# Attention on one core: the two parts of an output block are added by an accumulating DMA instead of by a Pool addition

## The chip, the cores and the metric

The kernel runs on one core of a Trainium2 chip. The core has TensorE (PE, matrix products), VectorE (DVE), ScalarE (ACT), GpSimd (Pool) and SyncE (SP), and 16 DMA engines that they share. SP and Pool both issue DMAs; a DMA that changes the type or accumulates is issued by Pool here. The metric is device time in microseconds. The kernel before takes 794.21 us, the median of three runs (793.92 to 794.26).

## The reference

For each of 8 batches the kernel computes softmax(q kT / sqrt(512)) v, in float32, with 2048 rows and 512 columns:

```python
scores = np.matmul(q, k.transpose(0, 2, 1)) / np.sqrt(d_k)
attn_weights = special.softmax(scores, axis=-1).astype(np.float32)
return np.matmul(attn_weights, v)
```

## The kernel before

*Tiling.* Each batch is worked through in four steps, g = 4b to 4b + 3, so g runs from 0 to 31. In a step TensorE computes half of the scores of the next span of 1024 query rows (class Group, product at L342) and, interleaved with that, the product of weights and values for four blocks of 128 output rows (classes Pair, L447, and Fine, L634). Both products use Strassen's scheme: seven block products in place of eight, with sums and differences of blocks made ahead by VectorE (L194 to L197 for k, L211 to L214 for q, L395 to L398 and L588 to L591 for the weights). For g = 1 to 29 the products named x, y and z of a pair are themselves done by an inner Strassen scheme, the function fine.

*Output.* Each Fine object has four quarters of its output: C11, C12, C21, C22, here o11, o12, o21 and o22, each 128 rows by 256 columns in float32. They are tiles of one pool of eight buffers (opool). ScalarE writes a quarter from PSUM with the row's factor (scaled, L456). For o11, there are two parts: the one from x is written to o11 by part(), and the one from y is written to a second tile, more, by after2(). Pool adds more to o11 at L555, and SP stores o11 to DRAM (store, L469). There are 58 of these additions: two in each of the steps g = 1 to 29. A step takes ten tiles of the pool. 

*Loads.* For the next batch, chunks of 512 rows of k, q and v are loaded by Pool's DMAs with a change from float32 to float16: k and q into a pool of two stage tiles (load, L133), v straight to its place (L220). SP transposes a stage tile into its place by a DMA transpose (L159). The transposed chunk of k is then summed by VectorE, L194 first (k_sums; the word k01 in the table is the first of the four sums for chunk 0).

*Order.* The order of everything is written out by hand. A step has 34 slots, and tables say what is put into each: PRODUCTS (t3@25 and t4@27 end in after2 for the pairs a and b), SUMS (k01@11 in the second step of a batch) and PLAN for loads and transposes:

```python
(0, 18, "load", "k", 0), (1, 0, "trans", "k", 0),
(0, 24, "load", "k", 1), (1, 8, "trans", "k", 1),
```

The first two numbers are the step of the batch and the slot. So on Pool the order around the end of a batch's first step is: load k0, load k1, addition a, addition b. On SP it is: store of o11 of a, store of o11 of b, transpose of k0, the stores of the o22 and o21 quarters, transpose of k1. Every engine works in the order in which its instructions were issued. An engine waits on semaphores where its data come from another engine or a DMA; these waits are put in by the framework.

Of the kernel before, what the change touches and what calls it, by code (L numbers as in the profile page):

```python
# [12 lines left out]
def kernel(  # L13
# [21 lines left out]
    nc = tc.nc  # L35
# [7 lines left out]
    ADD = mybir.AluOpType.add  # L43
# [266 lines left out]
    class Group:  # L310
# [61 lines left out]
        def after2(self):  # L372
            exp(self.left[0][:, self.j, :], self.y[:])
# [147 lines left out]
    class Fine(Pair):  # L521
# [29 lines left out]
        def after2(self):  # L551
            if "y" in INNER(self.g) and self.g < NP - 2:
                more = self.half()
                self.scaled(more, self.y[:, 0:H], self.r1)
                nc.gpsimd.tensor_add(self.o11, self.o11, more)  # L555
                self.store(self.o11, 0, slice(0, H))
                return
            if "y" in INNER(self.g):
                self.final(self.o11, self.y[:, 0:H], self.r1)
            else:  # L560
                self.o11 = self.half()
                self.scaled(self.o11, self.y[:, 0:H], self.r1)
            self.store(self.o11, 0, slice(0, H))
# [114 lines left out]
    def INNER(g):  # L678
        return INNERS[g % NQT] if 0 < g < NP - 2 else END_INNERS.get(g, "")
# [251 lines left out]
    for g in range(NP):  # L931
# [3 lines left out]
        more = sp < NP // 2  # L935
# [53 lines left out]
```

## Time and profile before

| What | Value |
|---|---|
| time, median of three runs (range) | 794.21 us (793.92 to 794.26) |
| profiled execution: span on the core | 792.4 us; the page gives no other time for it |
| busy: TensorE, VectorE, ScalarE, Pool | 786.1, 712.4, 646.3, 124.1 us |
| granted TensorE clock | 1.000 |
| HBM read, written | 100.73 MB, 33.55 MB |
| additions at L555 | 58, together 51.1 us of Pool |

The span runs from the first to the last instruction on the core. A row of a group has the line, the engine, the operation, the tiles (output, arrow, inputs), the shapes and the count; behind the bar stand the busy time in us, the mean of one in ns, and the idle time of the engine just before, with what ended it. A row of the timeline has the start in us, the duration in us, engine and line, and in brackets the idle time before and what ended it; instructions of the same kind that follow each other are merged, with their count. A row of the DMA issues has the count, the size of one and the median time in us from issue to landing. A queue's row has packets, megabytes, and the time that its packets took as a share of 16 engines over the span. In the waits, a row has the total in us, the count and the longest.

### The profile page before, as it was taken

Reading aid. Unit: us, or ns where it says so; the run is one execution under the profiler, and the core shown is the slowest. Engines: PE = TensorE matmul, PEld = TensorE weight load, DVE = VectorE, ACT = ScalarE, POOL = GpSimd, SP = SyncE. Lnnn points to the kernel's source line nnn. Section 1 sums busy time; section 2 is a strip of 40 time slices with the busy share of each in tenths; the row PEclk is TensorE's granted clock in tenths of the full one; section 3 lists DMA queues with packets and bytes.
Section 4 is the critical chain, followed back from the end, with each engine's and each line's share of the span. In section 5 each row is a group of like instructions: output and inputs, shape, how many; then the busy total and the mean of one; then the engine's idle time right before and its main releaser. Section 6 shows DMA issues by size and latency. Waiting matters only on the chain.

```text
span 792.4 us, 17987 instructions
## 1 busy us (share of the span) xinstructions
PE 786.1 (99%) x6574; PEld 536.6 (68%) x6574; DVE 712.4 (90%) x1562; ACT 646.3 (82%) x1339; POOL 124.1 (16%) x166
## 2 busy tenths in 40 slices
PE   9999999999999999999999999999999999999998
PEld 5556666666666666666666676666666666666686
DVE  3789999989999899998999989999899998999864
ACT  4678888888888888888988888888888888888862
POOL 4011111121121120211202121022210222100000
PEclk9999999999999999999999999999999999999999
DMA  9989991999929996399965999379991999911112
GB/s 222 180 149 187 159 192 35 175 199 166 180 43 186 209 176 134 71 195 180 172 130 106 193 189 180 82 136 200 163 202 55 151 195 178 195 35 47 49 66 95
DMA packets 206456, 116.05 MB, mean 146 GB/s; under 512 B 124320, under 2 KB 205344, under 8 KB 206368
## 3 DMA queue, kind: packets, MB, share of 16 engines
q0 software_dynamic: 49648, 49.29, 42.2%
q1 hardware_dynamic: 156432, 65.30, 39.0%
q8 instruction: 51, 0.84, 0.4%
q10 hardware_dynamic: 288, 0.33, 0.1%
q14 instruction: 37, 0.30, 0.1%
HBM read 100.73 MB, written 33.55 MB: 169 GB/s over the span
## 4 chain that ended last, share of the span: by engine, by line
PE 96%; DVE 2%; ACT 1%; issue 1%; DVEq 0%; ACTq 0%
PE t L342 45%; PE t L447 29%; PE t L634 17%; PE t L285 2%; DVE cz L367 1%; DVE ks L196 1%; PE tr L169 1%; PE tr L146 0%; PE t L853 0%; PE t L301 0%; DVE right L397 0%; ACT right L278 0%; ACT o L456 0%; ACT left L278 0%; DVE s L396 0%
## 5 line engine op out<-in xcount | busy, mean ns | idle before, releaser
L456 ACT ACTIVATE o<-t,r 128x256 f32<-128x256 f32 x314 | 143.9, 480 | 88.0 <-DVE r L482 33.2
L342 PE MATMUL t<-qraw,kraw 128*128 128x512 f16 x728 | 198.0, 379 | 0.1
L278 ACT ACTIVATE left<-t 128x512 f16<-128x512 f32 (+1 forms) x260 | 154.4, 601 | 12.0 <-PE t L342 5.8
L342 PE MATMUL t<-qs,ks 128*128 128x512 f16 x488 | 138.7, 379 | 0.1
L278 ACT ACTIVATE right<-cz 128x1024 f16<-128x1024 f32 x122 | 129.9, 1065 | 1.0 <-DVE cz L364 0.8
L342 PEld LDWEIGHTS <-kraw 128*128 128x128 f16 x976 | 87.1, 97 | 57.9 <-issue 0.6
L447 PEld LDWEIGHTS <-right 128*128 128x128 f16 x1024 | 99.5, 98 | 38.3 <-DVE right L397 2.7
L447 PEld LDWEIGHTS <-s 128*128 128x128 f16 x1072 | 102.1, 97 | 30.5 <-issue 0.3
L634 PEld LDWEIGHTS <-si 128*128 128x128 f16 x1044 | 75.4, 97 | 39.4 <-issue 1.4
L555 POOL TENSOR_TENSOR o<-o 128x256 f32<-128x256 f32 x58 | 51.1, 882 | 307.9 <-ACT o L456 221.2
L367 DVE TENSOR_TENSOR cz<-t,cz 128x512 f32<-128x512 f32 x122 | 83.8, 686 | 15.3 <-ACT o L456 6.7
L342 PEld LDWEIGHTS <-ks 128*128 128x128 f16 x732 | 67.9, 97 | 40.2 <-issue 0.2
L358 ACT COPY cz<-t 128x512 f32<-128x512 f32 x120 | 70.5, 587 | 26.2 <-PE t L342 25.2
L364 DVE TENSOR_TENSOR cz<-t,cz 128x512 f32<-128x512 f32 x122 | 83.5, 684 | 4.0 <-PE t L342 3.6
L634 PEld LDWEIGHTS <-left 128*128 128x128 f16 x928 | 66.2, 97 | 20.6
L459 DVE SCALAR_TENSOR_TENSOR o<-t,r,o 128x256 f32<-128x256 f32 x134 | 62.5, 478 | 19.0 <-ACT ci L652 6.4
L353 ACT COPY t<-t 128x512 f32<-128x512 f32 x120 | 69.9, 583 | 3.2 <-PE t L342 0.8
L447 PE MATMUL t<-vt,s 128*128 128x256 f16 (+1 forms) x560 | 72.5, 273 | 0.0
L342 PE MATMUL t<-qs,kraw 128*128 128x512 f16 x244 | 72.5, 378 | 0.0
L342 PE MATMUL t<-qraw,ks 128*128 128x512 f16 x244 | 72.4, 378 | 0.0
L361 ACT COPY cz<-t 128x512 f32<-128x512 f32 x122 | 71.2, 583 | 0.3
L634 PE MATMUL t<-vh,left 128*128 128x128 f16 x696 | 67.3, 219 | 0.0
(101 smaller groups left out, 1239.1 us busy)
## 6 DMA issues: line engine op xcount, KB each, us to landing
out_dram<-o SPq DMA_DIRECT2D x256, 128.0 KB, 2.5
vh<-in_v_dram POOLq DMA_DIRECT2D x32, 512.0 KB, 10.6
stage<-in_q_dram POOLq DMA_DIRECT2D x28, 512.0 KB, 7.1
stage<-in_k_dram POOLq DMA_DIRECT2D x28, 512.0 KB, 7.6
right<-in_q_dram POOLq DMA_DIRECT2D x2, 512.0 KB, 9.9
right<-in_k_dram POOLq DMA_DIRECT2D x2, 512.0 KB, 12.0
first<-in_q_dram SPq DMA_DIRECT2D x2, 256.0 KB, 3.7
cz<-in_q_dram SPq DMA_DIRECT2D x2, 256.0 KB, 4.7
```

The source lines that it names most:

```text
L278: nc.scalar.activation(out=out_, in_=in_, func=EXP, scale=inv_sqrt_d)
L342: nc.tensor.matmul(dst[:], lhs[:, j, dc, :], rhs[:, :, dc, :], start=(n in (1, 5) and dc == 0), stop=(dc == 1), skip_group_check=True,)
L353: f(out=self.y[:], in_=self.x[:])
L358: f(out=self.cz[:, 1, :], in_=self.z[:])
L361: nc.scalar.copy(out=self.cz[:, 0, :], in_=self.x[:])
L364: nc.vector.tensor_add(self.cz[:, 1, :], self.x[:], self.cz[:, 1, :])
L367: nc.vector.tensor_add(self.cz[:, 0, :], self.z[:], self.cz[:, 0, :])
L447: nc.tensor.matmul(dst[:, 0:width], lhs(j), rhs(j), start=(first and j == 0), stop=(j == NJ - 1), skip_group_check=True,)
L456: nc.scalar.activation(out=out_, in_=src, func=COPY, scale=r[:])
L459: nc.vector.scalar_tensor_tensor(out=out_, in0=src, scalar=r[:], in1=out_, op0=MULT, op1=ADD)
L555: nc.gpsimd.tensor_add(self.o11, self.o11, more)
L634: nc.tensor.matmul(dst, lhs[:, j, :], rhs[:, j, :], start=(n == 1 and j == 0), stop=(j == NI - 1), skip_group_check=True,)
```

## The change

In after2 the Pool instruction that adds more to o11 is replaced by a DMA that Pool issues. It reads more from SBUF, reads o11, and writes the sum to o11, in float32.

```diff
             if "y" in INNER(self.g) and self.g < NP - 2:
                 more = self.half()
                 self.scaled(more, self.y[:, 0:H], self.r1)
-                nc.gpsimd.tensor_add(self.o11, self.o11, more)
+                nc.gpsimd.dma_start(out=self.o11, in_=more, accum_op=ADD)
                 self.store(self.o11, 0, slice(0, H))
                 return
```

ADD is the addition that the kernel names at its start. The store that follows is issued by SP as before. Nothing else differs.

## The prediction

> **What bounds the kernel now.** I read the page's busy times and its chain first, then the row of the edited line, and after that the order in time on Pool, SP and VectorE around one of the edited places.
>
> ```profile
> span 792.4 us, 17987 instructions
> PE 786.1 (99%) x6574; PEld 536.6 (68%) x6574; DVE 712.4 (90%) x1562; ACT 646.3 (82%) x1339; POOL 124.1 (16%) x166
> PE 96%; DVE 2%; ACT 1%; issue 1%; DVEq 0%; ACTq 0%
> L555 POOL TENSOR_TENSOR o<-o 128x256 f32<-128x256 f32 x58 | 51.1, 882 | 307.9 <-ACT o L456 221.2
> ```
>
> TensorE is busy for 786.1 of 792.4 us and makes 96% of the chain. So at most 792.4 - 786.1 = 6.3 us could be won anywhere, and whatever stops TensorE is lost for good, for it has no idle time to catch up in. The 58 additions to be replaced (L555) take 51.1 us of Pool, which is 16% busy and not in the chain: taking them away is worth nothing by itself. The question is whether the accumulating DMA ends later than the addition did, and who stands behind it. The profiled execution has a span of 792.4 us; the median of the runs is 794.21, so 1.8 us lie around the span, and I add changes to 794.2.
>
> Who waits for L555 is seen in SP's own waits, and what SP does next in its timeline. This is the boundary between g = 8 and g = 9; g counts the groups of output rows, four to a batch, and I call them steps. Rows: start, duration, engine, line, operation, and in brackets the idle time before.
>
> ```profile
> SPq L469 <- POOL o L555: 68.8, 50, 2.6
> ...
> 250.41 7.04 SPq L469 DMA_DIRECT2D out_dram<-o  x4
> 257.56 3.81 SPq L159 DMA_TRANSPOSE kraw<-stage  x1
> 261.46 1.50 SPq L469 DMA_DIRECT2D out_dram<-o  x3
> ```
> ```profile
> 250.16 0.75 POOL L133 DMA_DIRECT2D stage<-in_k_dram  x1 [14.49 <-DMA qraw<-stage]
> 252.00 0.74 POOL L133 DMA_DIRECT2D stage<-in_k_dram  x1 [1.09 <-DMA qraw<-stage]
> 255.10 0.86 POOL L555 TENSOR_TENSOR o<-o 128x256 f32<-128x256 f32 x1 [2.36 <-issue]
> 256.18 0.92 POOL L555 TENSOR_TENSOR o<-o 128x256 f32<-128x256 f32 x1 [0.22 <-ACT o L456]
> ```
> ```profile
> 263.80 0.43 DVE L589 TENSOR_TENSOR si<-si,left 128x512 f16<-128x512 f16 x1
> 264.14 0.42 DVE L194 TENSOR_TENSOR ks<-kraw 128x512 f16<-128x512 f16 x1
> 265.53 0.69 DVE L367 TENSOR_TENSOR cz<-t,cz 128x512 f32<-128x512 f32 x1 [0.98 <-ACT o L456]
> ```
>
> Pool issues the loads of two key chunks (k0 at 250.16, k1 at 252.00), then makes the two additions. SP stores both sums, the last of the four stores before 257.56, and only then transposes k0. VectorE's first sum over k0 (L194) runs at 264.14, with no idle time ahead of it. The next rows are the landing times of k0's load, k1's load and k0's transpose.
>
> ```profile
> stage<-in_k_dram POOLq DMA_DIRECT2D x1, 512.0 KB, 7.3
> stage<-in_k_dram POOLq DMA_DIRECT2D x1, 512.0 KB, 8.8
> kraw<-stage SPq DMA_TRANSPOSE x1, 5.8
> ```
>
> k0's load lands at 250.16 + 7.3 = 257.5, and the transpose starts at 257.56: it lands at 263.4, and L194, which needs it, starts 0.8 us later. This is a chain without slack: load, transpose, sum.
>
> **The change part by part.** *Removed:* 58 Pool additions of 882 ns. *Added on Pool:* 58 DMA issues; the 512 KB loads above cost Pool 0.75 us each, so Pool is held about as long as before, and its later loads start as before: 0. *The sum of an output half* is no longer there 0.9 us after ScalarE wrote its second part, but when the DMA has landed. *SP's store* now waits for that landing, with everything behind it on SP: the other half's store, the transpose, the stores of the o22 and o21 halves.
>
> *When does it land?* Pool's DMAs all show as one queue, q0. Three loads, issued 0.76 us apart, show how it is served:
>
> ```profile
> 327.55 2.00 POOL L555 TENSOR_TENSOR o<-o 128x256 f32<-128x256 f32 x2 [21.86 <-ACT o L456]
> 329.50 1.52 POOL L133 DMA_DIRECT2D stage<-in_q_dram  x2
> 331.00 0.76 POOL L220 DMA_DIRECT2D vh<-in_v_dram  x1
> ```
> ```profile
> stage<-in_q_dram POOLq DMA_DIRECT2D x1, 512.0 KB, 6.5
> ...
> stage<-in_q_dram POOLq DMA_DIRECT2D x1, 512.0 KB, 9.8
> vh<-in_v_dram POOLq DMA_DIRECT2D x1, 512.0 KB, 12.7
> ```
>
> They land at 329.5 + 6.5 = 336.0, 330.3 + 9.8 = 340.1 and 331.0 + 12.7 = 343.7: one after the other, 4 us apart, not together. So the two accumulating DMAs, issued at about 255.1 and 256.2, stand behind k1's load, which lands at 252.00 + 8.8 = 260.8, 3.7 us after the last addition ended in the old kernel (256.18 + 0.92).
>
> *What does one take by itself?* No row shows an accumulating DMA. The queues' totals give the nearest packets:
>
> ```profile
> q0 software_dynamic: 49648, 49.29, 42.2%
> q1 hardware_dynamic: 156432, 65.30, 39.0%
> ```
>
> On q0 a packet of about 1 KB takes 0.422 x 16 x 792.4 / 49648 = 0.108 us, on q1 (smaller ones too) 0.032. An output half is 128 rows of 1 KB, 8 for each of 16 engines: 0.86 us at q0's price, 0.25 at q1's. Reading two operands and writing one without overlap may cost three times the first: 2.6. I take 0.86: it is Pool's own queue with rows of the same length; the ends are 0.25 and 2.6.
>
> *The sum for one place.* The transpose of k0 would start when k1's load has landed, plus two accumulating DMAs, plus the last store's issue (1.50 / 3 = 0.5 us by the row at 261.46). From that go the slack of L194 and the idle time of VectorE just after it, which takes up delay (0.98 us at 265.53). There are six such places, g = 4, 8, ... 24 with the next one (g = 0 has no L555, the last batch loads nothing). The first and the last of them, each with its k1 load, transpose, L194 and the L367 after it:
>
> ```profile
> 156.60 0.74 POOL L133 DMA_DIRECT2D stage<-in_k_dram  x1 [1.11 <-DMA qraw<-stage]
> ...
> stage<-in_k_dram POOLq DMA_DIRECT2D x1, 512.0 KB, 9.1
> ...
> 161.23 4.65 SPq L159 DMA_TRANSPOSE kraw<-stage  x1
> ...
> kraw<-stage SPq DMA_TRANSPOSE x1, 6.7
> ...
> 167.95 0.43 DVE L194 TENSOR_TENSOR ks<-kraw 128x512 f16<-128x512 f16 x1
> 169.16 0.69 DVE L367 TENSOR_TENSOR cz<-t,cz 128x512 f32<-128x512 f32 x1 [0.79 <-ACT o L456]
> ```
> ```profile
> 636.97 0.74 POOL L133 DMA_DIRECT2D stage<-in_k_dram  x1 [1.02 <-ACT cz L358]
> ...
> stage<-in_k_dram POOLq DMA_DIRECT2D x1, 512.0 KB, 7.6
> ...
> 641.97 3.29 SPq L159 DMA_TRANSPOSE kraw<-stage  x1
> ...
> kraw<-stage SPq DMA_TRANSPOSE x1, 6.8
> ...
> 648.84 0.43 DVE L194 TENSOR_TENSOR ks<-kraw 128x512 f16<-128x512 f16 x1 [0.21 <-DMA kraw<-stage]
> 649.94 0.69 DVE L367 TENSOR_TENSOR cz<-t,cz 128x512 f32<-128x512 f32 x1 [0.68 <-ACT o L456]
> ```
>
> k1's landing less the transpose's old start: 165.7 - 161.23 = 4.5, 260.8 - 257.56 = 3.2, 644.6 - 641.97 = 2.6; mean 3.4. Slack of L194: 0.0, 0.8, 0.1; mean 0.3; in the last place the sum waits for the transpose already. Idle time after it: 0.8, 1.0, 0.7; mean 0.8. So VectorE falls behind by 3.4 + 2 x 0.86 + 0.5 - 0.3 - 0.8 = 4.5 us in each place. What it does next (L367 and its like) frees the PSUM banks that TensorE writes, so I pass the whole delay on; a few tenths may be absorbed. 6 x 4.5 = 27; I take 26 for that and forecast 794.2 + 26 = 820 us. At the low end of the DMA's price the place costs 3.3 us (814), at the high end 8.0 (842).
>
> A page of the Trainium skill prices a transfer otherwise: "DMA: Bandwidth & Descriptors", section "Anatomy of one DMA — SWDGE (gpsimd) path", gives a DMA issued by Pool 2.0 us fixed and the bytes at 436 GB/s. By that one half would be 2.3 us, and if the fixed part were paid one after the other the forecast would be some 17 us higher, 837 (an estimate from that page). The rows above have no accumulating DMA to test it; three whole loads 4 us apart leave both open.
>
> *The other boundaries* are taken at 0. At the end of g = 9 no load is in the queue, so SP waits some 2 or 3 us longer; the chunk that is transposed next is summed half a step later. At the end of g = 10 a load of v is ahead, and the next transpose is one of q, read a step later. At the end of g = 11 (327.55) the two DMAs stand ahead of the three loads at 329.50: they put k0's chain off by up to 1.7 us if the queue is full, which would add 10 in all. The cover is that the queue was empty before them, so they run before the loads' packets come. *The output buffers*: ten halves are taken in a step and eight exist. ScalarE would stop if a store came so late that a half is not free; the stores behind the transpose are 6 us late. No DMA is among the rows that ScalarE waits for now, so I take 0, and with the slow DMA above it adds to the high end.
>
> **The rivals.**
> *The accumulating DMA is slow* (2.0 us or more each): 4.5 + 2 x (2.0 - 0.86) = 6.8 us in six places, 835, and 842 at 2.6; more if ScalarE runs out of output halves. For it speaks that reading the destination is new work; against it nothing in the trace. It begins to decide at about 1.5 us.
> *It does not stand behind the load:* packets of the two mix, and it lands some 3.5 us after issue (between the median 2.5 us of a 128 KB store to DRAM and the 6.5 us of a load).
>
> ```profile
> out_dram<-o SPq DMA_DIRECT2D x256, 128.0 KB, 2.5
> ```
>
> Then the transpose starts at 256.18 + 3.5 + 0.5 = 260.2, 2.6 late; less 0.3 and 0.8 that is 1.5 us, six times 9: 803. The three landings 4 us apart speak against it.
> *Hidden:* TensorE's and VectorE's leads take the whole delay: 794. Against it stands L194 with its slack of 0.0 to 0.8 us.
> *Faster:* Pool's additions read memory beside VectorE and slow it; without them VectorE is earlier and TensorE's last gaps close. At most the 6.3 us go, 788; it would decide if the SP wait cost under that. The page "SBUF — State Buffer" of the Trainium skill, section "Who interferes with whom", states such a shared port for VectorE instructions with two inputs in SBUF. The trace speaks against a gain that counts: VectorE is not what the chain runs over (2%).
>
> **How the numbers follow.** Chances: forecast 0.65, slow DMA 0.15, not behind the load 0.12, hidden 0.05, faster 0.03. The time is the first one's, 820; its own range, by the price of one DMA, is 810 to 832. The range for all, 802 to 842, takes in the rival at 803 and the bound at 842 and leaves about 2 in 10 out: hidden, faster, and the worse half of slow. What a measurement can tell from no change is 0.2%, 1.6 us: faster 0.03, same 0.05, slower 0.92.
>
> **What would show it.** In the new profile: SP's longest waits at L469 are for a DMA into o, of 5 to 8 us, six times; k0's transpose starts 5 to 6 us later against its load; VectorE shows idle time before L194 ended by the DMA kraw<-stage, some 4 to 5 us each, 25 to 30 in all; TensorE loses as much just after. The DMA's landing time is 6 to 8 us where a load is ahead, 3 to 4 elsewhere. Wrong would be: no wait before L194 (hidden or mixed), waits of ScalarE for out_dram stores (buffers), or a delay at every step and not at one in four (the DMA itself is slow).

## The result and the profile after

The changed kernel takes 818.59 us (median; 814.52 to 825.45) against 794.07 of the kernel before beside it: a ratio of 1.0317, with a 95% interval of 1.0268 to 1.0366. It is slower by some 25 us, inside the range of the forecast and 1.4 us from its number. The profiled execution has a span of 818.1 us, 25.7 more than before.

From the page and the list of waits (total in us, count, longest):

```profile
span 818.1 us, 18007 instructions
PE 792.2 (97%) x6574; PEld 542.7 (66%) x6574; DVE 697.7 (85%) x1562; ACT 645.1 (79%) x1339; POOL 124.2 (15%) x166
q0 software_dynamic: 58000, 56.90, 47.6%
PE 93%; DMA 4%; DVE 1%; ACT 1%; issue 0%; SPq 0%; ACTq 0%
L555 POOL DMA_DIRECT2D o<-o x58 | 50.4, 878 | 297.8 <-ACT o L456 263.5
```
```profile
DVE ks L194 <- DMA kraw<-stage: 31.4, 6, 7.4
PE t L634 <- DVE si L591: 20.4, 6, 5.5
SPq L469 <- DMA o<-o: 176.9, 50, 10.5
```

The chain now has 4% of DMA in it. VectorE waits six times for the transpose of k (31.4 us in all, 0.2 before), and TensorE six times for VectorE just after (20.4 us). Pool is held by a DMA issue about as long as by an addition, 878 ns against 882. One number goes the other way: VectorE is busy for 14.7 us less than before, with the same 1562 instructions.

The boundary between g = 8 and g = 9, in the timelines of Pool, SP, VectorE and TensorE:

```profile
255.34 0.74 POOL L133 DMA_DIRECT2D stage<-in_k_dram  x1 [2.83 <-DMA qraw<-stage]
256.08 1.82 POOL L555 DMA_DIRECT2D o<-o  x2
...
251.87 13.61 SPq L469 DMA_DIRECT2D out_dram<-o  x4
265.59 2.02 SPq L159 DMA_TRANSPOSE kraw<-stage  x1
...
271.53 0.42 DVE L194 TENSOR_TENSOR ks<-kraw 128x512 f16<-128x512 f16 x1 [7.38 <-DMA kraw<-stage]
...
273.68 0.61 PE L634 MATMUL t<-vh,si 128*128 128x128 f16 x4 [5.54 <-DVE si L591]
```

The DMA rows of that place are k1's load, the two accumulating DMAs and k0's transpose; then follow k0's transposes of the first and the fourth of the six places; the last row is an accumulating DMA at the end of a fourth step, with no load ahead of it:

```profile
stage<-in_k_dram POOLq DMA_DIRECT2D x1, 512.0 KB, 8.4
o<-o POOLq DMA_DIRECT2D x2, 128.0 KB, 8.4
kraw<-stage SPq DMA_TRANSPOSE x1, 5.9
...
kraw<-stage SPq DMA_TRANSPOSE x1, 4.2
kraw<-stage SPq DMA_TRANSPOSE x1, 4.3
...
o<-o POOLq DMA_DIRECT2D x1, 128.0 KB, 2.7
```

k1's load lands at 255.34 + 8.4 = 263.7. The accumulating DMAs were issued at 256.1 and 256.8 and land 8.4 us later, at 264.5 and 265.1: one after the other behind the load, 0.7 us each. Alone one takes 2.7 us. SP's store waits, the transpose starts at 265.59, and L194 waits 7.38 us for it.

### The profile page after: what moved, and what is told of

Its sections match the earlier page's. It is cut to its first block, busy times and chain, and to the rows that moved or that the text cites. A ratio compares the mean times of both kernels' runs of the same rounds, so it can differ in the third digit from the quotient of the medians.

```text
span 818.1 us, 18007 instructions
## 1 busy us (share of the span) xinstructions
PE 792.2 (97%) x6574; PEld 542.7 (66%) x6574; DVE 697.7 (85%) x1562; ACT 645.1 (79%) x1339; POOL 124.2 (15%) x166
## 4 chain that ended last, share of the span: by engine, by line
PE 93%; DMA 4%; DVE 1%; ACT 1%; issue 0%; SPq 0%; ACTq 0%
PE t L342 44%; PE t L447 30%; PE t L634 16%; DMA kraw<-stage 3%; PE t L285 2%; PE tr L169 1%; DMA first<-in_q_dram 1%; DVE cz L367 1%; PE t L301 0%; PE tr L146 0%; DVE left L590 0%; DVE si L591 0%; DVE t L658 0%; ACT left L278 0%; ACT right L278 0%
## 5 line engine op out<-in xcount | busy, mean ns | idle before, releaser
L342 PE MATMUL t<-qraw,kraw 128*128 128x512 f16 x728 | 198.1, 379 | 0.1
L342 PE MATMUL t<-qs,ks 128*128 128x512 f16 x488 | 141.7, 386 | 0.0
L342 PEld LDWEIGHTS <-kraw 128*128 128x128 f16 x976 | 87.3, 98 | 58.4 <-issue 1.7
L447 PEld LDWEIGHTS <-s 128*128 128x128 f16 x1072 | 104.5, 99 | 31.7 <-issue 0.9
L342 PEld LDWEIGHTS <-ks 128*128 128x128 f16 x732 | 68.9, 99 | 41.4 <-issue 2.6
L555 POOL DMA_DIRECT2D o<-o x58 | 50.4, 878 | 297.8 <-ACT o L456 263.5
L364 DVE TENSOR_TENSOR cz<-t,cz 128x512 f32<-128x512 f32 x122 | 83.8, 687 | 6.7 <-PE t L342 5.9
L634 PEld LDWEIGHTS <-left 128*128 128x128 f16 x928 | 68.3, 100 | 21.1
L342 PE MATMUL t<-qs,kraw 128*128 128x512 f16 x244 | 73.1, 381 | 0.0
L342 PE MATMUL t<-qraw,ks 128*128 128x512 f16 x244 | 72.5, 379 | 0.0
L447 PE MATMUL t<-vh,s 128*128 128x257 f16 x512 | 71.6, 285 | 0.0
```

The source lines that it names most:

```text
L342: nc.tensor.matmul(dst[:], lhs[:, j, dc, :], rhs[:, :, dc, :], start=(n in (1, 5) and dc == 0), stop=(dc == 1), skip_group_check=True,)
L364: nc.vector.tensor_add(self.cz[:, 1, :], self.x[:], self.cz[:, 1, :])
L447: nc.tensor.matmul(dst[:, 0:width], lhs(j), rhs(j), start=(first and j == 0), stop=(j == NJ - 1), skip_group_check=True,)
L555: nc.gpsimd.dma_start(out=self.o11, in_=more, accum_op=ADD)
L634: nc.tensor.matmul(dst, lhs[:, j, :], rhs[:, j, :], start=(n == 1 and j == 0), stop=(j == NI - 1), skip_group_check=True,)
```

## The experiments

The first four hold the forecast's theory A (the cost is SP's wait ahead of k0's transpose) against B (each accumulating DMA costs by itself).

**SP's order.** The transpose of k0 is put ahead of the two stores that wait.

```diff
-        (0, 18, "load", "k", 0), (1, 0, "trans", "k", 0),
-        (0, 24, "load", "k", 1), (1, 8, "trans", "k", 1),
+        (0, 18, "load", "k", 0),
+        (0, 24, "load", "k", 1), (0, 24, "trans", "k", 0), (1, 8, "trans", "k", 1),
```

> All 58 accumulating DMAs stay; only SP's order changes: the transpose of k0 is put ahead of the two stores of o11 that wait for them (end of the batch's first step). Theory A (the cost is SP's wait in front of that transpose, in six places): the 24 us go, 794 to 796 us, and VectorE shows no wait for kraw before L194. Rival B (the accumulating DMAs cost by themselves, each of 58, by their traffic, their landing time or late output buffers): it stays at 813 or more. Hidden third: ScalarE waits for output buffers, then some 800.

Measured: 799.30 us (795.32 to 806.16), ratio 1.0077 (1.0044 to 1.0110). Four fifths of the loss are gone with all 58 accumulating DMAs in place, so B falls. Some remains, near the 800 us of the third theory (late output buffers). The waits at L194, the DMA row of the transpose ahead of L194 near 558, and a row of ScalarE:

```profile
DVE ks L194 <- DMA kraw<-stage: 17.1, 6, 4.3
...
kraw<-stage SPq DMA_TRANSPOSE x1, 9.1
...
191.60 0.47 ACT L456 ACTIVATE o<-t,r 128x256 f32<-128x256 f32 x1 [2.32 <-DMA out_dram<-o]
```

The transpose starts on time now, but runs beside the rest of k1's load and the accumulating DMAs, and takes up to 9.1 us instead of the 5.8 to 6.8 shown of before. And ScalarE waits four times for a store, that is, for a free output buffer: 4.4 us in all, the longest 2.3. TensorE in turn waits 6.7 us for VectorE's L591 and 1.8 us for ScalarE, so late buffers are the smaller part of what remains.

**Pool's order.** The load of k1 is issued after the accumulating DMAs.

```diff
-        (0, 24, "load", "k", 1), (1, 8, "trans", "k", 1),
+        (0, 27, "load", "k", 1), (1, 8, "trans", "k", 1),
```

> All 58 accumulating DMAs stay and SP's order too; Pool issues the load of k1 after the two accumulating DMAs instead of before. A with a queue that is served in order: each lands some 2.7 to 2.9 us after issue (as in the steps without a load ahead) instead of 7 to 8, the transpose of k0 starts at about old + 2.0 us, less 0.3 slack and 0.8 idle time: 0.9 us in six places, 799 us (796 to 802). If the queue is not served in order and the DMA is slow at that time for other reasons: landing 6 us or more, 812 or more. B: 813 or more.

Measured: 811.06 us (807.97 to 816.90), ratio 1.0224 (1.0179 to 1.0269). A miss. The Pool timeline at the same boundary, the DMA rows of k0's load and of the two DMAs, the wait at L194, and a transpose of a later place:

```profile
251.92 0.74 POOL L133 DMA_DIRECT2D stage<-in_k_dram  x1 [15.47 <-DMA qraw<-stage]
255.81 0.90 POOL L555 DMA_DIRECT2D o<-o  x1 [3.14 <-ACT o L456]
...
stage<-in_k_dram POOLq DMA_DIRECT2D x1, 512.0 KB, 7.8
o<-o POOLq DMA_DIRECT2D x2, 128.0 KB, 4.6
...
DVE ks L194 <- DMA kraw<-stage: 27.0, 6, 5.8
...
kraw<-stage SPq DMA_TRANSPOSE x1, 8.0
```

k0's own load lands at 251.92 + 7.8 = 259.7 and is still ahead, so the two land 4.6 us after issue and not 2.8. And k1's load, moved back, now runs beside k0's transpose, which takes 8.0 us. What I had not reckoned with is that the length of a transpose depends on what runs beside it. The experiment agrees with a queue served in order but does not show the saving I had expected from that.

**The late transpose alone.** The kernel before, with Pool's additions, and k0's transpose seven slots later.

```diff
-        (0, 18, "load", "k", 0), (1, 0, "trans", "k", 0),
+        (0, 18, "load", "k", 0), (1, 7, "trans", "k", 0),
```

> The kernel before with Pool's additions, no accumulating DMA at all; the transpose of k0 is put seven slots later (slot 7 of the second step, behind the store of an o21 half). A: SP comes to it at about 263 in the timeline of before instead of 257.6, some 5.4 us late, which is what the accumulating DMAs do; 5.4 - 0.3 - 0.8 = 4.3 us in six places, 820 us (812 to 826). B, or a delay that VectorE's and TensorE's leads hide: 794 to 797.

Measured: 802.86 us (801.02 to 804.16), ratio 1.0111 (1.0094 to 1.0128): slower without any accumulating DMA, so the late transpose costs by itself, but 9 us and not the 26 of the expectation. The SP timeline, the transpose's DMA row, and L194:

```profile
262.91 4.46 SPq L159 DMA_TRANSPOSE kraw<-stage  x2
...
kraw<-stage SPq DMA_TRANSPOSE x1, 4.5
...
267.42 0.43 DVE L194 TENSOR_TENSOR ks<-kraw 128x512 f16<-128x512 f16 x1 [2.07 <-DMA kraw<-stage]
```

The start is 5.3 us later than before (257.56), as intended. But k1's load has landed by then, and the transpose takes 4.5 us where it took 5.8; L194 waits 2.07 us. In the six places VectorE waits 15.3 us at L194 and TensorE 6.5 us for L591.

**Only the first steps.** Accumulating DMAs at the end of each batch's first step alone, Pool additions elsewhere.

```diff
-                nc.gpsimd.dma_start(out=self.o11, in_=more, accum_op=ADD)
+                if self.g % NQT == 0:
+                    nc.gpsimd.dma_start(out=self.o11, in_=more, accum_op=ADD)
+                else:
+                    nc.gpsimd.tensor_add(self.o11, self.o11, more)
```

> Accumulating DMAs only in the first step of each batch (14 of the 58), Pool additions in the others. A: all of the loss is in these, 814 to 820 us. B: 14 of 58 parts of 24.5 us, 6 us, 800 us.

Measured: 807.16 us (804.54 to 810.61), ratio 1.0171 (1.0136 to 1.0205): 13 us, between the two. The wait at L194 is 22.3 us in the six places. Fourteen DMAs bring half of the loss, more than their share; the other half needs others as well.

**All but the first steps.** The same diff with != in place of ==.

> Accumulating DMAs in 44 places, Pool additions at the end of each batch's first step (14). Theory A (only SP's wait ahead of k0's transpose costs): 794 to 796 us. Theory C (A, and besides it the two accumulating DMAs at the end of a batch's fourth step stand ahead of q0's load and put the chain q0, k0, k0's transpose off by about 1.2 us): 796 to 799 us, with short waits of VectorE for kraw at L194. B (each of the 58 costs): 811 us or more.

Measured: 792.34 us (790.64 to 799.39), ratio 0.9984 (0.9965 to 1.0003): no slower than before, with 44 of the 58. **All but the fourth steps** has != 3 there:

> Accumulating DMAs in all steps but the fourth of each batch, which has Pool additions. C: k0's load comes at its old place against TensorE's work, the waits at L194 shrink by 1 us or more in five places, and the time comes to 807 to 813 us. A without C: unchanged, 816 to 820 us.

Measured: 808.06 us (806.03 to 809.26), ratio 1.0171 (1.0157 to 1.0185). The waits at L194 in the two, in this order:

```profile
DVE ks L194 <- DMA kraw<-stage: 8.3, 6, 2.3
```
```profile
DVE ks L194 <- DMA kraw<-stage: 23.0, 6, 4.3
```

So C holds: the DMAs at the end of the fourth step, ahead of q0's load, put the chain to k0 off. Alone that is nearly all absorbed: 8.3 us of VectorE's waits, 1.3 us of TensorE's, and no loss of time (a part of which is that these 44 places no longer pay for Pool's additions, see below). On top of the late transposes it takes the waits from 23.0 to 31.4 us and the time from 808 to 818, or to the 824.16 that the changed kernel took in the same series of runs. The two do not add up; they share one slack.

**Fillers.** What is a wait of 3 us worth to TensorE? The windows of 8 us behind each of the six waits of the changed kernel (columns: the window and its length; busy time and count of TensorE, its weight loads, VectorE, ScalarE and Pool; granted TensorE clock, DMA share, GB/s) say that the granted clock falls:

```profile
172.70:180.70 8.00, 8.00 (x72) 5.77 (x73) 6.60 (x18) 6.96 (x16) 0.74 (x1) 1.00 1.13 174
273.70:281.70 8.00, 8.00 (x55) 5.69 (x56) 5.09 (x17) 5.68 (x12) 0.74 (x1) 0.76 1.16 172
374.10:382.10 8.00, 8.00 (x43) 5.12 (x44) 4.12 (x14) 5.48 (x12) 0.74 (x1) 0.63 1.13 175
475.40:483.40 8.00, 7.98 (x56) 5.65 (x57) 5.32 (x17) 5.85 (x13) 1.13 (x2) 0.79 1.14 177
576.50:584.50 8.00, 7.96 (x49) 5.38 (x50) 4.63 (x15) 5.75 (x12) 0.74 (x1) 0.69 1.14 179
676.80:684.80 8.00, 7.96 (x56) 5.68 (x57) 5.32 (x17) 5.85 (x13) 0.74 (x1) 0.79 1.10 182
```

8 x (0.24 + 0.37 + 0.21 + 0.31 + 0.21) = 10.7 us of full clock are missing there, though TensorE is busy all the time. To take that away and leave the waits, products that nobody reads were put ahead of the product that waits:

```diff
     NS2 = 1
+    NFILL = 24
...
+        if part == 3 and s == 0 and g % NQT == 1 and 4 < g < NP - 6:
+            for _ in range(NFILL):
+                nc.tensor.matmul(
+                    xa[:, H + 8:512], vt2[:, 0, 0:P], vt1[:, 0, 0:H - 8],
+                    start=True, stop=True, skip_group_check=True,
+                )
```

> The changed kernel with 24 more matrix products of 248 columns in each of the six places, put directly ahead of the product that waits (results go to unused columns of a PSUM bank; the output is the same). They take about 2.5 us of each wait. If TensorE's half clock after the waits is a cost of its own: the granted clock stays at 1 in most places and the time falls to 807 to 812 us though as much work waits as before. If the half clock costs nothing that the chain feels: the same as the changed kernel beside it, 814 to 822 us; if the fillers themselves cost, more.

> The changed kernel as it is, beside the one with fillers: 814 to 825 us as before, with five or six waits at L194 and granted half clock after most of them.

Measured: 810.48 us (806.86 to 811.81) with fillers, 824.16 (817.14 to 826.88) without. Contrary to the first expectation the fillers change the output. So it was done again with start=False and nothing else different:

> As the kernel with 24 fillers, but these accumulate without a start mark, so that they touch nothing but the unused columns of the bank. The same time as with the start mark, 807 to 812 us, with the granted clock at 1 behind the waits; if the earlier time came from what the fillers did to the data, 814 to 825.

Measured: 809.02 us (807.61 to 810.63), ratio 1.0180 (1.0166 to 1.0194), and the output stays as it was, so it was the start mark that spoiled sums of the kernel. Granted clock, and the waits that are left:

```profile
core 0: 808.1 us, clock 1.000
...
DVE ks L195 <- DMA kraw<-stage: 30.8, 6, 6.4
PE t L635 <- DVE si L592: 4.7, 5, 2.0
```

VectorE waits as long as in the changed kernel (30.8 against 31.4 us), there are 144 products more, and the kernel is 10 to 15 us faster. The half clock behind the waits is a cost of its own.

**No addition.** VectorE's 14.7 us pointed to the rival that I had given 0.03. The kernel before without the addition shows what Pool's additions cost in all:

```diff
-                nc.gpsimd.tensor_add(self.o11, self.o11, more)
```

> The kernel before with no addition at all: the second part of o11 is computed by ScalarE but left out of the output (o11 is stored with its x part alone). Nothing takes the addition's place. G: VectorE's busy time falls from 712 to about 698 us, and the time to 788 to 791.5 us, which is the most that moving the addition off Pool could win. Without G: 794, VectorE's busy time as before.

Measured: 788.84 us (788.08 to 789.16), ratio 0.9925 (0.9913 to 0.9938). VectorE's rows for two of its sums (mean in ns last before the second bar), before, after the change, and without addition:

```profile
L213 DVE TENSOR_TENSOR qraw<-qraw 128x1024 f16<-128x1024 f16 x15 | 16.0, 1067 | 0.0
L588 DVE TENSOR_TENSOR si<-s 128x512 f16<-128x512 f16 x29 | 15.8, 545 | 0.2
```
```profile
L213 DVE TENSOR_TENSOR qraw<-qraw 128x1024 f16<-128x1024 f16 x15 | 10.3, 685 | 0.0
L588 DVE TENSOR_TENSOR si<-s 128x512 f16<-128x512 f16 x29 | 12.2, 422 | 0.2
```
```profile
PE 781.5 (99%) x6574; PEld 538.0 (68%) x6574; DVE 697.7 (89%) x1562; ACT 644.2 (82%) x1339; POOL 72.5 (9%) x108
L213 DVE TENSOR_TENSOR qraw<-qraw 128x1024 f16<-128x1024 f16 x15 | 10.2, 683 | 0.0
```

The mean of L213 was 1067 ns with Pool's additions in the kernel and is 685 or 683 without. Taken one by one in the kernel before, the 13 sums of L213 that overlap an addition take 1.02 to 1.22 us and the other two 0.68; of L588, seven take 0.94 us and 22 that overlap none 0.41 to 0.43. L364, which has one of its two inputs in PSUM, takes 685 ns with an addition beside it and 684 without.

In all the additions cost 5.6 us of the kernel's time (794.39 - 788.84). TensorE's weight loads show the way it takes. These waits for VectorE's sums stand in the list of the kernel before, 5.2 us together; without the additions none of them is left, nor in the changed kernel. Without the additions the span falls from 792.4 to 787.2, by the same 5.2 us:

```profile
PEld L447 <- DVE right L397: 2.7, 7, 0.4
PEld L634 <- DVE si L589: 1.3, 7, 0.2
PEld L634 <- DVE si L588: 1.2, 7, 0.2
```

**A version that beats both.** Accumulating DMAs where they do not bear on k0's chain, at the ends of the second and third steps:

```diff
-                nc.gpsimd.dma_start(out=self.o11, in_=more, accum_op=ADD)
+                if self.g % NQT in (1, 2):
+                    nc.gpsimd.dma_start(out=self.o11, in_=more, accum_op=ADD)
+                else:
+                    nc.gpsimd.tensor_add(self.o11, self.o11, more)
```

> Accumulating DMAs only at the ends of the second and third step of each batch (g mod 4 is 1 or 2), Pool additions at the two ends that bear on k0's chain. Theory G (a Pool addition makes VectorE instructions beside it longer, and without it TensorE waits less) with A and C: no waits at L194 and a small gain, 789.5 to 792.5 us, with a smaller spread than with DMAs in all steps but the first. Without G: 794 to 795.

Measured: 792.46 us (790.88 to 793.25), ratio 0.9971 (0.9961 to 0.9982): 1.9 us faster than the kernel before.

## Why the prediction was right, and where it was not

The mechanism and the place were right: a queue served in order, SP's store behind it, k0's transpose behind the store, L194 with no slack; no wait elsewhere in TensorE's list. That the number came within 1.4 us of the median is in part luck, because errors cancelled.

| Step | Forecast | Measured |
|---|---|---|
| two DMAs behind the load, one place | 1.7 us | 1.4 us (263.7 to 265.1) |
| k0's transpose | as long as before, 5.8 to 6.8 us | 4.2 or 4.3 in four places, 5.9 and 5.2 in the second and fifth |
| DMAs at the end of the fourth step | 0, at most 10 in all | they bring 10 to 16 us on top of the rest (808 to 818 or 824) |
| VectorE's waits, six places | 6 x 5.3 = 32 us; 27 with the idle time behind L194 taken off | 31.4 us |
| TensorE takes the delay on | all of the 27 us | 20.4 us of waits |
| half clock behind the waits | not in the sum | 10.7 us |
| Pool's additions gone | 0 | -5.6 us (by the kernel without them) |

TensorE's 20.4 + 10.7 - 5.6 make 25.5 us, and the span grew by 25.7. That sum takes the price of the additions from another kernel. Two rows bear it out: against the kernel without additions, TensorE's idle time grows by 20.2 us (from 787.2 - 781.5 to 818.1 - 792.2) and its busy time by 10.7; and the fillers with start=False, which take away the half clock alone, should give 794.4 + 20.4 - 5.6 = 809.2 and gave 809.02.

What cancelled is this. Over the six places k0's transposes took 28.1 us, 9.1 less than before, and the DMAs at the end of the fourth steps, put at 0, added 8.4 us to VectorE's waits (31.4 - 23.0). TensorE waited 11.0 us less than VectorE, 1.8 us less in each place, where the forecast took off 0.8; and the half clock, which no term of the sum had, cost 10.7.

The step "taking them away is worth nothing by itself" failed, and with it the sentence that the trace speaks against a gain that counts because the chain runs over VectorE for only 2%. The 6.3 us that I took for the most that could be won were read from TensorE's busy time, and that time is no floor: it fell from 786.1 to 781.5 us with the same 6574 products, with the same mean of a product (379 ns for the two largest groups, L342, in both). Products overlap in its rows, so that short waits between them count as busy. The rival's mechanism is at work in the changed kernel too; its gain is only smaller than the new wait. By the page "SBUF — State Buffer" of the Trainium skill, section "Who interferes with whom", a VectorE instruction with two SBUF inputs and a Pool instruction that reads SBUF shut each other out; the 1067 and 685 ns agree, and so does L364, which has one input in SBUF alone.

"At the end of g = 11 ... I take 0" failed too: those DMAs do put k0's chain off, by 8.3 us of VectorE's waits when they come alone; that cost no time there, but it did once the transpose was late as well. The prediction's estimate of 837, for DMAs that pay a fixed time one after the other, is refuted: two that follow each other are 0.7 us apart. The expectation for the late transpose alone missed by 17 us for two reasons: the transpose's length was taken as fixed (it was 4.5 us where it had been 5.8), and TensorE was taken to lose all that VectorE waits (it lost 6.5 of 15.3 us).

Why the loss in the kernel with SP's other order is 5 us and not 0 is told by the long transposes and the buffer waits, and TensorE's own waits give the shares: 6.7 us behind the first, 1.8 behind the second. The half clock came once, for 3.41 us from 561.1 on, which is 1.7 us of full clock. 6.7 + 1.8 + 1.7 - 5.6 = 4.6, and the span grew by 5.3 (797.7 against 792.4).

## What to carry to other kernels

An operation moved from an engine to a DMA was done here not when it was issued but after everything ahead in that queue had landed; look for what stands ahead of it there, and for the in-order queue that will wait for it with other work behind. Price a wait of TensorE with the half clock that can follow it, and do not take a transfer's length as fixed when you move it beside other transfers. An off-path engine can still be a cost by slowing its neighbour; compare the mean duration of the same instruction with and without it.

## What the runs showed of the hardware

A wait of TensorE can be followed by a stretch of reduced clock. The first and the last of the six waits of the changed kernel, in TensorE's timeline:

```profile
172.66 0.40 PE L634 MATMUL t<-vh,si 128*128 128x128 f16 x4 [2.37 <-DVE si L591]
...
676.84 0.53 PE L634 MATMUL t<-vh,si 128*128 128x128 f16 x4 [2.48 <-DVE si L591]
```

After the one of 2.37 us the granted clock over 8 us was 1.00, after the one of 2.48 us it was 0.79. The changed kernel's times scatter over 11 us, the kernel's before over 0.6; in the first four executions the granted clock is 0.991 in the fastest (814.52 us) and 0.979 in the slowest (825.45).

The Trainium skill's page "TensorE: Matmul & The Clock Gate", section "Part 1: The HAM clock gate (the "warmup" mystery)", tells of a free-running window of about 3.4 us in which activity is counted. This case's traces agree: in the profiled execution of the changed kernel the clock is halved from 270.8, 373.2, 475.6, 574.6 and 677.0 us on, for 3.41 or 6.83 us each time, and these starts lie 102.4, 102.4, 99.0 and 102.4 us apart, which is 30, 30, 29 and 30 times 3.413. On that grid the first wait falls into two windows, and the last one whole into one (columns as above):

```profile
168.38:171.79 3.41, 1.91 (x18) 1.06 (x16) 1.25 (x4) 0.84 (x2) 0.74 (x1) 1.00 0.94 230
171.79:175.21 3.42, 2.56 (x25) 1.95 (x26) 3.21 (x12) 2.51 (x8) 0.81 (x2) 1.00 1.12 149
...
673.55:676.96 3.41, 0.93 (x6) 0.32 (x5) 2.24 (x7) 0.80 (x3) 1.55 (x2) 1.00 0.94 228
676.96:680.37 3.41, 3.41 (x22) 2.56 (x21) 1.82 (x8) 1.62 (x5) 0.00 (x0) 0.50 0.93 140
```

The first wait leaves 1.5 us (3.41 - 1.91) and 0.9 us of a window idle, and the clock stays; the last leaves 2.5 us of one window idle, and the next window has the half clock. All 13 traces of this case, read window by window from 30 us on to shortly before the end, draw the same line: after a window at full clock with 1.98 us or more idle the half clock came each time (19 windows), and with 1.86 us or less it never came. So a wait much shorter than the window sufficed, and where it falls decides. That this makes the whole scatter is inferred; no run shifted the waits and nothing else.

An accumulating DMA of 128 KB within SBUF lands 2.7 us after its issue when nothing is ahead, costs its queue 0.7 us, and holds Pool for 0.88 us. A DMA transpose of one chunk of k took 4.2 us in the changed kernel's first place, and up to 9.1 us beside a load and two accumulating DMAs.
